# GpSimd issues the transfers of its own weights, and its second vector's product has a tile apart from the staging tile

## The chip, the core and the metric

The kernel is one program on one core of a Trainium2 chip. The core has five engines with an instruction queue each: TensorE (PE in the profile; PEld are its weight loads), VectorE (DVE), ScalarE (ACT), GpSimd (POOL) and SyncE (SP). Transfers between the chip's memory (HBM) and the on-chip memory (SBUF) run on 16 DMA engines, and an instruction in the queue of one of the engines starts each of them. The metric is device time in microseconds for one execution, smaller is better. For the kernel before, three runs gave 1352.70, 1353.47 and 1354.14 us, with a median of 1353.47 us.

## The reference

Two blocks of two layers each run one after the other on 256 tokens of width 1024, all in fp32. In both blocks a conditioning vector makes a shift, a scale and a gate for the channels; this is the *modulation*, and it is the part of the computation that the change touches.

```python
def hybrid_layer(x, c_silu, ...):                  # block 1, two layers
    mod = c_silu @ w_ada + b_ada                   # one vector x [1024, 3072]
    shift, scale, gate = jnp.split(mod, 3, axis=-1)
    u = rms_norm(x, norm_g) * (1 + scale[:, None]) + shift[:, None]
    z = u @ w_in                                   # then three attentions with their gates
    ...
    return x + gate[:, None] * (merged @ w_out)

def mixer_layer(x, cx, c, c_ctx, ...):             # block 2, two layers
    shift, scale, gate = jnp.split(jax.nn.silu(c) @ w_ada + b_ada, 3, axis=-1)
    shift_c, scale_c, gate_c = jnp.split(jax.nn.silu(c_ctx) @ w_ada + b_ada, 3, axis=-1)
    h = x * (1.0 + scale[:, None]) + shift[:, None]
    hc = cx * (1.0 + scale_c) + shift_c
    ...                                            # h @ w_in, hc @ w_in, then four mixers A, B, C, D
    x_new = layer_norm(alpha * x + gate[:, None] * (y @ w_out), ln_g, ln_b)
```

In block 1 one vector goes through `w_ada`, in block 2 two of them do (that of the tokens and that of the context).

## The kernel before, in words

Activations lie in SBUF with channels on the 128 partitions. The large products are fp32-exact by splitting: `raw` (L215 to L224) brings half a weight tile, [128, 4, 256] or 512 KB, into one of three buffers `wr` by a DMA on SP's queue (L222); `wtile` (L226) splits it into a rounded half `wh` (ACT, L114) and a remainder `wl` (DVE, L115); and TensorE makes three products per slice (L107) into PSUM. A load may be issued when a `wr` buffer is free, which is when the `wl` of the tile three loads earlier is done. All loads stand in the one queue of SP and are issued in its order.

The modulation products are background work. `ada` (L289) makes two sorts of it: `job` (TensorE multiplies the weights by the vector) and `wide` (L317), which leaves the multiplication to GpSimd. A `wide` fetches four chunks of 512 KB into `wsp` tiles (L324), and per chunk and 128-row slice GpSimd scales the slice by one entry of the vector (L330 the first, L333 the others) and adds it to the accumulator `acc` (L334). With two vectors (block 2) the first vector's product needs a tile of its own, `wc`, while the second's overwrites the weights. The `wsp` tiles take turns in a list of tags, `N.spare`: two buffers, `t3a` and `t3b` (L1373), which the jobs at the very start have used before, and eight where layer 2 of block 1 begins (`fill`, L256 and L539). `wc` lies in the tag `stg`, which has one buffer and is also the staging tile of `queries` and `quads` (L450, L461); these fill it on ACT and DVE and send it on by DMA.

When the accumulator is full, `end` (L336) lets TensorE sum over the partitions (`acc` against `ones`) and DVE write the result to `mod` (L342). `run_later` (L245) puts that 6 or 10 weight tiles after the wide. There are ten wides, six with one vector and four with two, so L324 stands for 40 transfers.

Two other things stand in GpSimd's queue: the `pow` operations of the norms, among them that of `rstd_row` (L379). At the start of a layer of block 1, DVE writes `rc` (L378), GpSimd raises it (L379), DVE makes the diagonal `dg` from it (L382), TensorE spreads it (L107), DVE copies it to `rstd` (L385) and scales the activations (L524), ACT writes `uh` (L525), and with that the layer's first projection can begin.

The order in each engine's queue is not the order of the Python code alone: the program is built with a scheduler that simulates engines and queues while it places instructions (`schedule_with_timeline_sim=True`, L1487), so an edit in one place can move instructions in another. The last part of the program that the prediction speaks of is mixer C of block 2 (`diff`, L1000), whose softmax per head alternates between TensorE, DVE (L482, L1019 to L1021) and ACT (L487, L497).

Of the kernel before, what the change touches and what calls it, by code (L numbers as in the profile page):

```python
# [58 lines left out]
class Net:  # L59
# [229 lines left out]
    def ada(self, l, blk):  # L289

        nc = self.nc
        nv = 1 if blk == 1 else 2
        wa = self.I["w_ada" if blk == 1 else "w_ada_2"][l]
        v0 = blk - 1
        mod = self.const.tile([128, 24, nv], F32, name=f"mod{blk}{l}")

        def load(n):
            return [self.raw(wa, k, n * 256, 256, True) for k in (0, 4)]

        def job(n, ws=None):  # L300
            ws = ws or load(n)
            bias = self.colB[:, 48 * (blk - 1) + 24 * l:48 * (blk - 1) + 24 * l + 24]
            p = self.P(self.pj, [128, 512])
            for k in range(8):
                g = 32 * (k % 4)
                self.mm(p[g:g + 32, :256], self.cs[:, k, :], ws[k // 4][:, k % 4, :], start=k < 4, stop=k >= 4)
            sb = self.W("adas", [128, 256], tag="score")
            nc.scalar.activation(sb, p[:, :256], AF.Copy)
            pc = self.P(self.tr, [128, 2, 4, 32])
            for j in range(2):  # L310
                self.T(pc[:, j].rearrange("p g v -> p (g v)"), sb[:, 128 * j:128 * j + 128])
            r = self.W("adar", [128, 2, nv])
            nc.vector.tensor_reduce(r, pc[:, :, :, v0:v0 + nv].rearrange("p j g v -> p j v g"), axis=AX.X, op=OP.add)
            nc.vector.scalar_tensor_tensor(mod[:, 2 * n:2 * n + 2, :], r, 0.5,
                                           bias[:, 2 * n:2 * n + 2][:, :, None].to_broadcast([128, 2, nv]),
                                           op0=OP.mult, op1=OP.add)
        def wide(n, tag):  # L317

            P = nc.gpsimd
            acc = self.K("acc", [128, 2, 512], tag=tag)  # L320
            for c in range(4):
                w = self.K("wsp", [128, 2, 512], tag=self.spare[self.nspare % len(self.spare)])
                self.nspare += 1
                nc.sync.dma_start(out=w, in_=wa[256 * c:256 * c + 256, 512 * n:512 * n + 512].rearrange(  # L324
                    "(k p) n -> p k n", p=128))
                for k in range(2):
                    for v in range(nv):
                        m = self.cs[:, 2 * c + k, v0 + v:v0 + v + 1]
                        if c == k == 0:
                            P.tensor_scalar(acc[:, v], w[:, k], m, None, op0=OP.mult)  # L330
                        else:
                            t = self.W("wc", [128, 512], tag="stg") if v + 1 < nv else w[:, k]
                            P.tensor_scalar(t, w[:, k], m, None, op0=OP.mult)  # L333
                            P.tensor_tensor(acc[:, v], acc[:, v], t, op=OP.add)  # L334

            def end():  # L336
                p = self.P(self.tr, [128, 4, 32])
                for j in range(4):
                    for v in range(nv):
                        self.mm(p[:, j, v:v + 1], acc[:, v, 128 * j:128 * j + 128], self.ones[:, 0:1])  # L340
                bias = self.colB[:, 48 * (blk - 1) + 24 * l:48 * (blk - 1) + 24 * l + 24]
                nc.vector.scalar_tensor_tensor(mod[:, 4 * n:4 * n + 4, :], p[:, :, :nv], 0.5,  # L342
                                               bias[:, 4 * n:4 * n + 4][:, :, None].to_broadcast([128, 4, nv]),
                                               op0=OP.mult, op1=OP.add)
            self.later.append((6 if nv == 1 else 10, end))

        return (mod, [lambda ws=None, n=n: job(n, ws) for n in range(12)], [lambda n=n: wide(n, ("s4", "w1")[n % 2]) for n in range(6)],
                load)

# [1142 lines left out]
```

## Time and profile before

| | |
|---|---|
| median of three runs | 1353.47 us (1352.70 to 1354.14) |
| the profiled execution | 1352.58 us, of which its span is 1350.8 us |
| TensorE busy | 1277.5 us, 95% of the span |
| VectorE busy | 908.9 us, 67% |
| ScalarE busy | 648.8 us, 48% |
| GpSimd busy | 393.9 us, 29%, nearly all of it before 660 us |
| mean granted TensorE clock | 0.972 of full speed |
| DMA | 217.65 MB in the span |

The trace is of one execution. Its span runs from the first instruction to the last, and 1.78 us of the execution lie around it. That execution was 0.89 us faster than the median. A sum made against the profiled execution therefore starts from 1352.6 us. Busy shares are averages over stages with different limits, so the rows below are read by stretches of the span.

### The profile page before, as it was taken

The page shows a single profiled execution, that of the slowest core. Times are in us where ns is not written, and L with a number is a line of the kernel's source. Part 1 is how long each engine was busy: PE and PEld are TensorE (multiplying, and loading weights), DVE is VectorE, ACT ScalarE, POOL GpSimd, SP SyncE. Part 2 cuts the span into 40 slices and gives each one's busy share as a digit, 9 for nine tenths or more (in the row PEclk, how much of TensorE's full clock was granted, in tenths as well). Part 3 has the DMA queues.
Part 4 walks back from the last instruction along what each step waited for, and adds up shares of the span by engine and source line. Part 5 has one row for each costly group of instructions (what it writes and reads, how often), then busy time and mean ns, then how long its engine had stood idle before and what let it go on. Part 6 is the DMA issues. An engine that isn't in the chain of part 4 may idle for free.

```text
span 1350.8 us, 27852 instructions
## 1 busy us (share of the span) xinstructions
PE 1277.5 (95%) x11386; PEld 1163.7 (86%) x11386; DVE 908.9 (67%) x1717; ACT 648.8 (48%) x1160; POOL 393.9 (29%) x233
## 2 busy tenths in 40 slices
PE   6999999999998999999998999999899999999986
PEld 2988988999898898899997988987789789999775
DVE  3897675665679855486675376754748768696873
ACT  3445456644444545764453233334736646434652
POOL 0484984150098921949500010000000000000000
PEclk8899999999989999999998999999899998999997
DMA  9764885476645575446664554326244255654220
GB/s 327 252 203 141 250 244 166 137 243 211 179 143 170 150 209 161 141 155 209 208 208 142 155 157 133 91 94 172 77 142 140 74 161 156 188 159 109 79 79 32
DMA packets 199599, 217.65 MB, mean 161 GB/s; under 512 B 10800, under 2 KB 183472, under 8 KB 198832
## 3 DMA queue, kind: packets, MB, share of 16 engines
q1 hardware_dynamic: 199472, 215.87, 53.2%
q8 instruction: 90, 1.47, 0.5%
q14 instruction: 37, 0.30, 0.1%
HBM read 199.06 MB, written 4.19 MB: 150 GB/s over the span
## 4 chain that ended last, share of the span: by engine, by line
PE 72%; DVE 12%; issue 6%; SPq 4%; DMA 3%; ACT 3%; POOL 0%; POOLq 0%; ACTq 0%; DVEq 0%
PE ps L107 68%; PE ps L111 4%; DVE wl L115 3%; SPq L466 2%; DMA wr<-w_in 2%; SPq L222 1%; DVE pe L703 1%; DVE nm L482 1%; DVE score L589 1%; ACT pe L487 1%; DMA wsp<-w_ada 1%; ACT wh L114 1%; DVE m L588 1%; DVE ro L428 1%; DVE score L584 0%
## 5 line engine op out<-in xcount | busy, mean ns | idle before, releaser
L115 DVE TENSOR_TENSOR wl<-wr,wh 128x1024 fp32r<-128x1024 f32 (+1 forms) x270 | 357.6, 1326 | 226.9 <-ACT wh L114 223.3
L114 ACT ACTIVATE wh<-wr 128x1024 fp32r<-128x1024 f32 (+1 forms) x270 | 284.9, 1056 | 349.3 <-PE ps L107 200.0
L107 PE MATMUL ps<-uh,wh 128*128 128x256 f32 x704 | 201.8, 287 | 3.4 <-ACT thm L659 3.4
L107 PE MATMUL ps<-ul,wh 128*128 128x256 f32 x704 | 201.2, 286 | 0.0
L107 PE MATMUL ps<-uh,wl 128*128 128x256 f32 x704 | 200.7, 285 | 0.0
L333 POOL TENSOR_SCALAR wsp<-wsp,cs 128x512 f32<-128x512 f32 x70 | 137.3, 1967 | 20.9 <-DMA wsp<-w_ada 20.9
L107 PEld LDWEIGHTS ps<-uh,wh 128*128 128x128 f32 x704 | 132.8, 189 | 5.8 <-ACT thm L659 4.4
L107 PEld LDWEIGHTS ps<-ul,wh 128*128 128x128 f32 x704 | 132.7, 188 | 3.1 <-issue 2.9
L107 PEld LDWEIGHTS ps<-uh,wl 128*128 128x128 f32 x704 | 132.8, 189 | 1.5 <-issue 1.1
L107 PE MATMUL ps<-wh,uh 128*128 128x256 f32 (+1 forms) x416 | 121.3, 293 | 1.8 <-ACT uh L525 1.4
L107 PE MATMUL ps<-wl,uh 128*128 128x256 f32 (+1 forms) x416 | 121.0, 292 | 1.5 <-DVE wl L115 1.5
L107 PE MATMUL ps<-wh,ul 128*128 128x256 f32 (+1 forms) x416 | 120.4, 290 | 0.4 <-DVE ul L526 0.4
L334 POOL TENSOR_TENSOR acc<-acc,wsp 128x512 f32<-128x512 f32 x70 | 107.8, 1540 | 2.5
L487 ACT ACTIVATE pe<-ps,nm 128x512 f32<-128x512 f32 (+2 forms) x160 | 85.0, 542 | 42.3 <-DVE nm L482 29.3
L397 POOL TENSOR_TENSOR rec<-rec,mhalf 128x8 f32<-128x8 f32 (+1 forms) x10 | 15.4, 1544 | 293.9 <-DVE rec L396 193.8
L482 DVE TENSOR_REDUCE nm<-ps 128x1 f32<-128x512 f32 (+2 forms) x104 | 70.8, 685 | 26.3 <-PE ps L107 24.7
L107 PEld LDWEIGHTS ps<-wh,uh 128*128 128x128 f32 x416 | 82.1, 198 | 3.7 <-ACT uh L525 1.6
L107 PEld LDWEIGHTS ps<-wl,uh 128*128 128x128 f32 x416 | 82.2, 198 | 2.8 <-DVE wl L115 1.8
L107 PEld LDWEIGHTS ps<-wh,ul 128*128 128x128 f32 x416 | 82.1, 198 | 0.8 <-DVE ul L526 0.7
L379 POOL TENSOR_TENSOR rc<-rc,mhalf 128x2 f32<-128x2 f32 x6 | 5.0, 833 | 255.4 <-DVE rc L378 255.4
L107 PE MATMUL ps<-wl,hxh 128*128 128x256 f32 x256 | 73.2, 286 | 0.5 <-DVE wl L115 0.5
L107 PE MATMUL ps<-wh,hxh 128*128 128x256 f32 x256 | 73.2, 286 | 0.1
(377 smaller groups left out, 3526.3 us busy)
## 6 DMA issues: line engine op xcount, KB each, us to landing
wr<-w_in SPq DMA_DIRECT2D x204, 512.0 KB, 4.1
wsp<-w_ada SPq DMA_DIRECT2D x68, 512.0 KB, 5.0
wr<-w_out SPq DMA_DIRECT2D x40, 512.0 KB, 3.5
wr<-w_ada SPq DMA_DIRECT2D x28, 512.0 KB, 4.5
wr<-w_br_a SPq DMA_DIRECT2D x8, 512.0 KB, 3.6
wr<-w_br_c SPq DMA_DIRECT2D x8, 512.0 KB, 4.0
wr<-w_br_b SPq DMA_DIRECT2D x8, 512.0 KB, 4.3
kC<-stg SPq DMA_DIRECT2D x64, 64.0 KB, 2.1
```

What stands on the lines that cost most here:

```text
L107: self.last_mm = self.nc.tensor.matmul(o, l, r, start=start, stop=stop, skip_group_check=True).ins
L111: self.nc.tensor.transpose(o, i, self.ident[:n, :n])
L114: self.nc.scalar.activation(h, x, AF.Copy)
L115: self.nc.vector.tensor_tensor(l, x, h, op=OP.subtract)
L222: self.nc.sync.dma_start(out=w[:, :, :n], in_=ap[k0 * 128:k0 * 128 + 512, c0:c0 + n].rearrange("(k p) n -> p k n", p=128))
L333: P.tensor_scalar(t, w[:, k], m, None, op0=OP.mult)
L334: P.tensor_tensor(acc[:, v], acc[:, v], t, op=OP.add)
L397: self.nc.gpsimd.tensor_tensor(r, r, self.mhalf[:, :r.shape[1]], op=OP.pow)
L428: V.tensor_tensor(dst, t1, b, op=OP.add)
L466: self.nc.sync.dma_start(out=d[32 * i:32 * i + 32].bitcast(F32), in_=g[32 * j:32 * j + 32, part].bitcast(F32))
L482: nc.vector.tensor_reduce(nmx, p, axis=AX.X, op=OP.max, negate=True)
L487: nc.scalar.activation(e[:, j, :], p[:, j, :], AF.Exp, bias=nm[:, h:h + 1], accum_out=ss[:, h:h + 1])
```

## The change

The transfers of `wide` are issued from GpSimd's queue instead of SP's, and `wc` gets the tag `w2` in the pool of long-lived tiles. That tag is otherwise used once, by a tile of the second layer of block 2.

```diff
             for c in range(4):
                 w = self.K("wsp", [128, 2, 512], tag=self.spare[self.nspare % len(self.spare)])
                 self.nspare += 1
-                nc.sync.dma_start(out=w, in_=wa[256 * c:256 * c + 256, 512 * n:512 * n + 512].rearrange(
+                P.dma_start(out=w, in_=wa[256 * c:256 * c + 256, 512 * n:512 * n + 512].rearrange(
                     "(k p) n -> p k n", p=128))
...
-                            t = self.W("wc", [128, 512], tag="stg") if v + 1 < nv else w[:, k]
+                            t = self.K("wc", [128, 512], tag="w2") if v + 1 < nv else w[:, k]
                             P.tensor_scalar(t, w[:, k], m, None, op0=OP.mult)
                             P.tensor_tensor(acc[:, v], acc[:, v], t, op=OP.add)
```

The three places in the order of the instructions on which the prediction rests follow. A row has the number on its engine, the line, the operation, the tiles it writes and reads, and in the first two pieces the semaphores that it waits for (DMAHW a transfer issued by SP, DMASW one issued by GpSimd, the others engines).

GpSimd's queue at the start of the program, before the change (`rc` is the norm's small tile, `wsp` a weight chunk, `acc` the accumulator):

```order
7 L379 TENSOR_TENSOR rc<-rc,mhalf 128x2 [waits DVE_49]
8 L330 TENSOR_SCALAR acc<-wsp,cs 128x512 [waits DMAHW6_49]
9 L333 TENSOR_SCALAR wsp<-wsp,cs 128x512 [waits DMAHW1_49,DMAHW0_49,PE_49]
10 L333 TENSOR_SCALAR wsp<-wsp,cs 128x512 [waits DMAHW2_49,DMAHW7_49,DMAHW1_49,PE_49]
11 L333 TENSOR_SCALAR wsp<-wsp,cs 128x512
12 L334 TENSOR_TENSOR acc<-acc,wsp 128x512 [waits Pool_49] x3
```

And after it:

```order
7 L379 TENSOR_TENSOR rc<-rc,mhalf 128x2 [waits DVE_49]
8 L324 DMA wsp<-w_ada 128x2x512 [waits DMAHW1_49,DMAHW0_49,PE_49]
9 L324 DMA wsp<-w_ada 128x2x512 [waits DMAHW2_49,DMAHW1_49,PE_49]
10 L330 TENSOR_SCALAR acc<-wsp,cs 128x512 [waits DMASW0_49]
11 L333 TENSOR_SCALAR wsp<-wsp,cs 128x512
12 L333 TENSOR_SCALAR wsp<-wsp,cs 128x512 [waits DMASW1_49]
13 L333 TENSOR_SCALAR wsp<-wsp,cs 128x512
14 L334 TENSOR_TENSOR acc<-acc,wsp 128x512 [waits Pool_49] x2
15 L324 DMA wsp<-w_ada 128x2x512
```

The first two transfers now stand right behind the first `pow` and wait only for the jobs that used `t3a` and `t3b`, no longer for the loads that stood ahead of them in SP's queue; later transfers stand between GpSimd's own operations.

GpSimd's queue where block 1's second layer begins, before the change:

```order
72 L334 TENSOR_TENSOR acc<-acc,wsp 128x512 [waits Pool_49] x3
73 L379 TENSOR_TENSOR rc<-rc,mhalf 128x2 [waits DVE_49]
74 L330 TENSOR_SCALAR acc<-wsp,cs 128x512 [waits DMAHW0_49,PE_49]
75 L330 TENSOR_SCALAR acc<-wsp,cs 128x512
76 L333 TENSOR_SCALAR wc<-wsp,cs 128x512 [waits DMAHW6_49,DMAHW7_49,DMAHW5_49,Activation_49]
```

And after it:

```order
108 L334 TENSOR_TENSOR acc<-acc,wsp 128x512 [waits Pool_49] x3
109 L324 DMA wsp<-w_ada 128x2x512 [waits DMAHW0_49,PE_49]
110 L324 DMA wsp<-w_ada 128x2x512 [waits DMAHW2_49,PE_49,Pool_49]
111 L379 TENSOR_TENSOR rc<-rc,mhalf 128x2 [waits DVE_49]
112 L330 TENSOR_SCALAR acc<-wsp,cs 128x512 [waits DMASW0_49]
113 L330 TENSOR_SCALAR acc<-wsp,cs 128x512
114 L333 TENSOR_SCALAR wc<-wsp,cs 128x512
```

Two transfers now stand ahead of the norm's `pow` in GpSimd's queue, and they wait for TensorE; and the first `wc` no longer waits for the three transfers out of the staging tile.

VectorE's queue in mixer C of the last layer, before the change (L482, L1019, L1020 and L1021 are the softmax of a head, L115 is the `wl` of a weight tile):

```order
1302 L1020 SCALAR_TENSOR_TENSOR dc<-ss,nlam,dc 128x1
1303 L482 TENSOR_REDUCE nm<-ps 128x1
1304 L1021 SCALAR_TENSOR_TENSOR pe<-pe,dc 128x512
1305 L482 TENSOR_REDUCE nm<-ps 128x1
1306 L1019 RECIPROCAL dc<-ss 128x1
1307 L1020 SCALAR_TENSOR_TENSOR dc<-ss,nlam,dc 128x1
1308 L482 TENSOR_REDUCE nm<-ps 128x1
1309 L1021 SCALAR_TENSOR_TENSOR pe<-pe,dc 128x512
```

And after it:

```order
1304 L1021 SCALAR_TENSOR_TENSOR pe<-pe,dc 128x512
1305 L482 TENSOR_REDUCE nm<-ps 128x1
1306 L115 TENSOR_TENSOR wl<-wr,wh 128x1024
1307 L1019 RECIPROCAL dc<-ss 128x1
1308 L1020 SCALAR_TENSOR_TENSOR dc<-ss,nlam,dc 128x1
1309 L482 TENSOR_REDUCE nm<-ps 128x1
1310 L1021 SCALAR_TENSOR_TENSOR pe<-pe,dc 128x512
1311 L482 TENSOR_REDUCE nm<-ps 128x1
1312 L115 TENSOR_TENSOR wl<-wr,wh 128x1024
```

Weight tiles are now split between the heads. TensorE's queue has the counterpart: before, the last eight of the fourteen gaps between the heads' score products hold no projection product; now six of these eight hold 3 to 14 each, 66 in all, which stood further ahead.

## Rows read from the trace of the kernel before

**Rows 1.** Busy time of an engine, its share of the span and its instructions.

```profile
PE 1277.5 (95%) x11386; PEld 1163.7 (86%) x11386; DVE 908.9 (67%) x1717; ACT 648.8 (48%) x1160; POOL 393.9 (29%) x233
```

**Rows 2.** Busy time by stretch: us, each engine (instructions), granted clock, DMA share, GB/s.

```profile
45.00:120.00 75.00, 72.04 (x567) 66.99 (x566) 69.13 (x127) 34.48 (x67) 55.53 (x33) 0.98 0.64 191
120.00:290.00 170.00, 167.98 (x1347) 156.27 (x1348) 105.85 (x148) 93.14 (x155) 101.59 (x57) 1.00 0.66 200
...
400.00:470.00 70.00, 65.86 (x515) 59.02 (x514) 66.48 (x119) 33.52 (x68) 65.38 (x38) 1.00 0.51 151
470.00:660.00 190.00, 187.06 (x1518) 176.61 (x1517) 113.84 (x150) 102.10 (x157) 116.81 (x66) 1.00 0.60 178
```

**Rows 3.** SP queue's waits: line, waited for, us in total, times, longest.

```profile
SPq L324 <- POOL acc L334: 57.7, 23, 6.8
```

**Rows 4.** Waits of all engines: the one of GpSimd for the staging tile.

```profile
POOL wc L333 <- DMA bq<-stg: 47.6, 1, 47.6
```

**Rows 5.** Costliest groups, GpSimd's two: count, busy, mean ns, idle before.

```profile
L333 POOL TENSOR_SCALAR wsp<-wsp,cs 128x512 f32<-128x512 f32 x70 | 137.3, 1967 | 20.9 <-DMA wsp<-w_ada 20.9
...
L334 POOL TENSOR_TENSOR acc<-acc,wsp 128x512 f32<-128x512 f32 x70 | 107.8, 1540 | 2.5
```

**Rows 6.** Timeline of GpSimd, end of the last accumulation: start us, us.

```profile
657.60 1.30 POOL L334 TENSOR_TENSOR acc<-acc,wsp 128x512 f32<-128x512 f32 x1
```

**Rows 7.** Timeline of TensorE, that accumulator's sum over the partitions.

```profile
678.69 1.84 PE L107 MATMUL ps<-ones,acc 128*128 128x1 f32 x16
```

**Rows 8.** Timeline of SP's queue at the start.

```profile
37.58 1.51 SPq L324 DMA_DIRECT2D wsp<-w_ada  x2
39.18 18.23 SPq L222 DMA_DIRECT2D wr<-w_in  x5
...
59.27 0.37 SPq L222 DMA_DIRECT2D wr<-w_in  x1
```

**Rows 9.** Timeline of TensorE at the start.

```profile
28.21 1.08 PE L107 MATMUL ps<-wsp,cs 128*32 128x256 f32 x8
...
30.48 1.94 PE L107 MATMUL ps<-wsp,cs 128*32 128x256 f32 x16
...
36.36 0.58 PE L107 MATMUL ps<-wl,uh 128*128 128x256 f32 x1 [1.48 <-DVE wl L115]
```

**Rows 10.** Busy time by stretch at the start.

```profile
30.00:35.00 5.00, 3.90 (x22) 1.49 (x22) 2.22 (x9) 2.22 (x5) 0.00 (x0) 0.50 1.09 349
```

**Rows 11.** Timeline of GpSimd at the start.

```profile
45.99 1.84 POOL L330 TENSOR_SCALAR acc<-wsp,cs 128x512 f32<-128x512 f32 x1 [26.50 <-DMA wsp<-w_ada]
```

**Rows 12.** Timeline of VectorE, two splits without and with GpSimd at work.

```profile
38.15 2.35 DVE L115 TENSOR_TENSOR wl<-pre,wh 128x1024 fp32r<-128x1024 f32 x2
...
54.73 4.51 DVE L115 TENSOR_TENSOR wl<-wr,wh 128x1024 fp32r<-128x1024 f32 x2
```

**Rows 13.** Timeline of all engines where block 1's second layer begins.

```profile
366.93 0.88 SPq L324 DMA_DIRECT2D wsp<-w_ada  x2
...
367.88 0.16 DVE L378 TENSOR_SCALAR rc<-ps 128x2 f32<-128x2 f32 x1 [1.18 <-PE ps L107]
368.12 0.73 POOL L379 TENSOR_TENSOR rc<-rc,mhalf 128x2 f32<-128x2 f32 x1 [78.45 <-DVE rc L378]
...
371.70 0.51 PE L107 MATMUL ps<-wh,uh 128*128 128x256 f32 x2 [1.36 <-ACT uh L525]
```

**Rows 14.** Busy time by stretch in the last layer's mixers.

```profile
1265.00:1280.00 15.00, 12.90 (x81) 9.60 (x81) 12.64 (x27) 11.37 (x27) 0.00 (x0) 1.00 0.22 70
```

**Rows 15.** Timeline of TensorE in mixer C of the last layer.

```profile
1273.24 1.10 PE L107 MATMUL ps<-vC,pt 128*128 128x64 f32 x8
1274.16 0.47 PE L107 MATMUL ps<-kC,qCx 128*128 128x512 f32 x1
...
1275.53 0.50 PE L107 MATMUL ps<-kC,qCx 128*128 128x512 f32 x1 [0.15 <-ACT pe L487]
1276.06 1.10 PE L107 MATMUL ps<-vC,pt 128*128 128x64 f32 x8
```

## The prediction

> **What bounds the kernel now.** I read the busy times first: TensorE works 1277.5 us, 95% of the span, and GpSimd 393.9, 29% [rows 1]. So an edit on GpSimd and SP can gain only where TensorE stands idle, and I looked at the stretches in which GpSimd accumulates [rows 2]. The reader is to see how little TensorE loses there: 2.96 us in 45 to 120, 2.02 in 120 to 290, 4.14 in 400 to 470 and 2.94 in 470 to 660, 12.1 us in all. That is the most that any relief of SP's queue could give, whatever else causes these losses. In 400 to 470 two other engines are full too, DVE with 66.48 and GpSimd with 65.38 of 70 us.
>
> Then the waits. SP's queue stands 57.7 us, in 23 waits, at L324, because a `wsp` buffer is still being multiplied [rows 3]; every `wr` load behind it is late by that much. It is the wait that the change takes away from SP. But the three `wr` buffers lie between, and in 120 to 290, where GpSimd accumulates for 101.59 us, TensorE is busy 167.98 of 170. GpSimd stands 47.6 us, once, for the staging tile [rows 4]. What waits for GpSimd there is only its own accumulator, and that is not in a hurry: the last one is complete at 658.9 us (657.60 + 1.30) [rows 6] and TensorE sums it at 678.69 [rows 7], 19.8 us later; it is the tightest of the ones I compared.
>
> **The price of an issue.** The trace holds no transfer issued by GpSimd. An issue on SP took 0.37 us [rows 8]; that is the lower end. GpSimd's smallest operation, on 128x2 elements, took 0.73 us [rows 13], so every instruction there carries a fixed part; 0.37 + 0.73 = 1.1 us is my value. A full GpSimd operation on 512 columns averages 1.97 us [rows 5], an upper end if writing an issue costs as much as computing. Further off lies the case that GpSimd stays with a transfer until it has landed: the pair issued at 37.58 let GpSimd start at 45.99 [rows 8, 11], 8.4 us for two, so 4.2 us each.
>
> **The change part by part**, against the profiled execution's 1352.6 us (its span of 1350.8 and 1.8 around it; 0.9 under the median).
>
> *SP's queue freed.* 40 issues leave SP: 40 x 0.37 = 15 us of its time, beside the 57.7 us of waits. Cover: the `wr` buffers, and SP would next wait for `wl` instead of for GpSimd. Value 0; the gain's end is the idle time above, worked out as a rival.
>
> *The tile `wc` off the staging tag.* 47.6 us of GpSimd wait go; they lie in the stretch before an accumulator that has tens of microseconds. Value 0.
>
> *Issues between GpSimd's own operations.* Four per wide, 4 x 1.1 = 4.4 us, against a slack of at least 19.8 us. Value 0. If an issue cost 4.2 us, four would take 16.8 us, which is still inside.
>
> *A, the start of the program: +1.5 us (0 to +5.2).* In SP's queue the first two transfers stood behind the first weights and the constants and went out at 37.58 [rows 8]. Now they need only the jobs that used the two buffers, which end at 29.3 and about 32 us (28.21 + 1.08; 30.48 + 1.94) [rows 9]. There the DMA engines are full, 349 GB/s [rows 10], with the loads that the first projections wait for. Two transfers of 0.524 MB are 1.05 MB / 349 GB/s = 3.0 us. If all of it came ahead of the first weights, the projections would begin 3.0 us later; with alternating packets half of that; 0 if the wait for DVE at 36.36 [rows 9] covers it. I take half. GpSimd's first products then come at about 36 to 38 instead of 45.99 [rows 11] and meet the first splits on DVE. Two splits took 2.35 us with GpSimd idle and 4.51 us with it at work [rows 12], 2.2 us more; that is added to the upper end alone, because the same meeting takes place later in the kernel before.
>
> *B, the layer boundary: +1.0 us (0 to +7.2).* SP issued the two transfers of the next wide at 366.93 (TensorE frees the buffer), and GpSimd was free for `rc` at 368.12, right behind DVE's write at 367.88 [rows 13]. Now both issues stand ahead of `rc`: 366.93 + 2 x 1.1 = 369.1, so `rc` begins 1.0 us later. Queued behind it are `dg`, the sum on TensorE, `rstd`, `uh` and the projection at 371.70, which had no other work to hide in. At 0.37 us an issue is over by 367.7 and costs nothing; at 1.97 it is 366.93 + 3.94 - 368.12 = +2.75; at 4.2, +7.2.
>
> *C, mixer C of the last layer: -2.1 us (-4 to +2).* From 1265 to 1280 TensorE is busy 12.90 of 15 us, DVE 12.64 [rows 14]. A head takes 2.82 us (1273.24 to 1276.06), and TensorE waits in it for ACT's exponentials [rows 15]. Now 66 projection products lie in these gaps. The idle 2.10 us are filled by work that stood in a stretch without idle time, so they come off the end. The busy figures of waiting products may hide as much again: -4. Against it: each head has a split of 1.2 us (half of the 2.35) more on DVE, 2.82 to 4.0 us per head; 28 products fill about that, but the last two heads are bare as before. If DVE sets the pace and the products don't cover it, two heads lose 1 us each: +2.
>
> *D, 400 to 470: -1.0 us (-3 to +1).* DVE has 95% there, slowed by GpSimd as in [rows 12]. Eight issues, 8.8 us, in which GpSimd writes no tile, spread its work thinner; part of the stretch's 4.14 idle TensorE us comes back. I take a quarter.
>
> Sum: 1.5 + 1.0 - 2.1 - 1.0 = -0.6, so 1352.0 by the profiled execution, 1352.9 by the median. I forecast 1352.4: no change that can be told.
>
> Two rules of the Trainium skill stand against or beside this. The rows show DVE and GpSimd slowing each other [rows 12]. The page "SBUF — State Buffer", section "SBUF: two separate sides", says more: a transfer issued from GpSimd has its descriptors written by GpSimd, and while DVE runs an operation that takes both port pairs these can't be written, so such loads belong in SP's or ACT's queue. No run so far shows it for an issue. At the boundary it would hold an issue up by a short operation of DVE, 0.48 us at the longest, for a sum of about -0.1 in place of -0.6; it gets no weight of its own. And "DMA: Bandwidth & Descriptors", section "Issuing engines are not separate DMA queues", says that another issuing engine saves only the time that the queue takes to issue. TensorE's 167.98 of 170 us with a blocked SP agree, and by it the freed queue is worth 0, as above.
>
> **The rivals.**
>
> 1. *GpSimd's issues hold up the norm (slower).* B with an issue near 4.2 us instead of 1.1. For it: GpSimd's waits behind two issues in one queue, and nothing else to do on TensorE. Against: SP's own 0.37. It decides from about 3.2 us an issue: 366.93 + 6.4 - 368.12 = +5.2, so 1352.0 + 4.2 = 1356.2. At 4.2 the time is 1352.0 - 1.0 + 7.2 = 1358.2; if the start goes the same way (A at +3), 1359.7. Chance 0.18.
> 2. *Thinner contention (faster).* The idle 4.14 us of 400 to 470 all come back: 1352.0 - 3.1 = 1348.9. For it: both engines full there; against: the work of GpSimd is the same, only later. Chance 0.13.
> 3. *SP was the limit after all (faster).* Half of the 7.9 us lost in the other three stretches comes back: 1352.0 - 4 = 1348.0. For it the 57.7 us; against it the full TensorE and the DMA share of 0.6. Chance 0.12.
> 4. *The heads don't gain.* DVE's splits cost what the filling gives, C at +2: 1352.0 + 4.1 = 1356.1. Chance 0.07.
>
> **How the numbers follow.** The forecast has 0.50, its own range 1349 to 1356. About 0.2%, 2.7 us, can be told from no change: faster is under 1350.8, slower over 1356.2. Of the forecast's 0.50, 0.38 is no change, 0.09 faster, 0.03 slower; rivals 2 and 3 are faster; rival 1 gives 0.15 slower and 0.03 no change, rival 4 gives 0.04 and 0.03. Faster 0.34, no change 0.44, slower 0.22. The range of 1346 to 1358.5 takes in both faster rivals and rival 1 up to its price of 4.2 us, and leaves some 0.08 below and 0.10 above.
>
> **What would show it.** The idle of TensorE in 120 to 290 and 470 to 660 should stay near 2 and 3 us with the wait of 57.7 us gone from SP's queue, and SP's waits for `wl` grow. At the start, GpSimd's first product should begin at 36 to 38 us, the first projection up to 3 us later. At the boundary the rows give the price directly: two issues, then `rc`; if `rc` begins within 0.3 us behind DVE's write, B is wrong, if 4 us behind it, rival 1 is right. In mixer C of the last layer TensorE should be full but for two heads. The wait for the staging tile should be gone without a trace on TensorE. The forecast is wrong if TensorE's sums over `acc` wait for GpSimd, or if DVE's splits grow beside GpSimd's issues.

## The result: slower by 1.0%

| | kernel before | changed kernel |
|---|---|---|
| median | 1354.14 us (5 runs, 1352.70 to 1355.08) | 1369.89 us (5 runs, 1361.28 to 1375.52) |
| ratio | | 1.010, 95% interval 1.0075 to 1.0124 |
| profiled execution, its span | 1352.58, 1350.8 us | 1361.28, 1359.1 us |
| mean granted TensorE clock | 0.972 | 0.970 there; 0.962 to 0.970 over the five |

I forecast 1352.4 us and a range up to 1358.5; that was wrong. The changed kernel is not only slower, it scatters: its five executions lie 14 us apart, those of the kernel before 2.4 us. The profiled one is the fastest of the five, so its trace shows only a part of the loss; the experiments show the rest. A ratio here and below is taken over the runs within 1.5% of their kernel's fastest, so it can differ from the quotient of the medians, which are of all runs; a trace of a run beyond that is not used.

The page of the changed kernel, its busy times, its new DMA queue and GpSimd's transfers (packets, MB and share; then count, KB, us from issue to landing):

```profile
PE 1280.4 (94%) x11386; PEld 1167.7 (86%) x11386; DVE 899.0 (66%) x1717; ACT 647.1 (48%) x1160; POOL 424.3 (31%) x273
...
q0 software_dynamic: 5760, 20.97, 5.1%
...
wsp<-w_ada POOLq DMA_DIRECT2D x40, 512.0 KB, 5.1
```

Busy time by stretch, to compare with [rows 2], and the largest wait of SP's queue:

```profile
120.00:290.00 170.00, 168.19 (x1328) 154.72 (x1327) 98.90 (x151) 94.26 (x164) 90.46 (x63) 0.99 0.63 185
470.00:660.00 190.00, 187.03 (x1498) 175.10 (x1497) 118.55 (x160) 103.55 (x165) 132.12 (x82) 0.99 0.60 177
```

```profile
SPq L222 <- DVE wl L115: 533.5, 179, 16.7
```

The same wait in the kernel before:

```profile
SPq L222 <- DVE wl L115: 483.3, 180, 13.2
```

The change does what it says: 40 transfers left SP, and their wait of 57.7 us [rows 3] is gone. It was worth nothing in the two stretches where GpSimd accumulates and TensorE is the busiest: TensorE is busy 168.19 of 170 and 187.03 of 190 us, after 167.98 and 187.06. SP waits instead for `wl`, 533.5 us against 483.3 before. (The stretches are of equal time, not of equal work; the later ones begin some 10 us of work earlier than in [rows 2].)

**Where the time goes.** ACT writes a `wh` tile 274 times, and I set the beginnings of these splits in one trace beside those in the other. Up to the first (33 us) the traces agree within 0.2 us. Between the 1st and the 11th, 33 to 61 us in the kernel before, the changed kernel loses 8.9 us. To the 93rd (359 us) it loses 5.3 more, to the 126th (496 us, with the boundary and the rope of layer 2) it gains 2.8, and to the 271st (1311 us) it gains 2.3.

Most of the 5.3 us go at 110 to 120 us, where the granted clock is 0.50 for 10.2 us, behind a stop of TensorE of 2.17 us. In the kernel before TensorE stops at the same work for 1.57 us, and no such fall follows. This part comes and goes with the execution: three of the kernels below (issue only, late product, first four on SP) have the same 10.2 us and lose 3.8 to 5.0 us between these splits; a repeat of the changed kernel has none and loses nothing there; the kernel with the tile alone has 6.8 us of it and loses 1.1.

The start first. GpSimd and DVE, then TensorE, each from its timeline (start, duration, what is written and read, idle time before and what ended it):

```profile
29.97 0.91 POOL L324 DMA_DIRECT2D wsp<-w_ada  x1 [10.19 <-DMA wsp<-w_ada]
32.22 0.73 POOL L324 DMA_DIRECT2D wsp<-w_ada  x1 [1.34 <-PE ps L107]
36.88 3.03 POOL L330 TENSOR_SCALAR acc<-wsp,cs 128x512 f32<-128x512 f32 x1 [3.94 <-DMA wsp<-w_ada]
...
49.37 0.77 POOL L324 DMA_DIRECT2D wsp<-w_ada  x1
```

```profile
48.21 1.51 DVE L115 TENSOR_TENSOR wl<-pre,wh 128x272 fp32r<-128x272 f32 x1
49.65 1.88 DVE L191 TENSOR_TENSOR nlam<-lamsm 128x1 f32<-128x1 f32 x2
51.45 0.68 DVE L428 TENSOR_TENSOR ro<-ro,rt 128x512 f32<-128x512 f32 x1
```

The same three of DVE in the kernel before, and TensorE in the changed one:

```profile
45.96 0.43 DVE L115 TENSOR_TENSOR wl<-pre,wh 128x272 fp32r<-128x272 f32 x1
46.31 0.65 DVE L191 TENSOR_TENSOR nlam<-lamsm 128x1 f32<-128x1 f32 x2
46.88 0.68 DVE L428 TENSOR_TENSOR ro<-ro,rt 128x512 f32<-128x512 f32 x1
```

```profile
52.28 1.08 PE L111 MATMUL ps<-ident,ro 128*128 128x128 f32 x4 [2.31 <-DVE nlam L193]
```

An issue takes 0.91 or 0.73 us. The first two go out at 29.97 and 32.22, against 37.58 [rows 8], and GpSimd multiplies from 36.88 on, 9 us earlier than in [rows 11]. That is as forecast. DVE then is late in its chain of small operations: `ro` (L428) begins at 51.45, and TensorE stands 2.31 us for it (the row names `nlam`, a neighbour of `ro` on DVE; the products read `ro`). In the kernel before, the same `ro` began at 46.88 and TensorE didn't stand. The 4.6 us have two causes. The constants landed later, behind the two transfers (the last of them at 45.41 against 43.07). And DVE's operations ran beside GpSimd's: the small `wl` at 48.21 took 1.51 us, 0.43 before; the two `nlam` 1.88 us, 0.65 before. One of the `nlam`, at 49.65, began inside the issue of the third transfer (49.37) and was let in only behind the accumulation that followed it: 1.7 of the 4.6 us hang on an issue and the operation behind it, not on a product.

What I hadn't counted is what follows the stop. Busy time by stretch again, granted clock third from the right, and below it one row of the kernel before:

```profile
50.00:55.00 5.00, 2.72 (x14) 2.75 (x14) 4.35 (x8) 1.54 (x2) 3.48 (x4) 0.72 0.69 180
55.00:60.00 5.00, 5.00 (x25) 5.00 (x25) 2.55 (x4) 1.06 (x1) 5.00 (x4) 0.50 0.75 239
60.00:65.00 5.00, 5.00 (x25) 5.00 (x25) 1.16 (x1) 1.09 (x2) 4.92 (x4) 0.50 0.34 105
65.00:70.00 5.00, 5.00 (x28) 5.00 (x27) 2.71 (x5) 0.86 (x3) 3.10 (x4) 0.57 0.68 209
```

```profile
55.00:60.00 5.00, 5.00 (x32) 5.00 (x32) 4.97 (x6) 1.72 (x3) 3.08 (x2) 0.66 0.57 170
```

After the stop TensorE is busy without a gap, but the granted clock is 0.50 (1.2 GHz of 2.4) for 17.1 us, up to 69 us. In the kernel before, it was at that level for 3.4 us between 55 and 60. The 13.7 us more cost about half of that, 6.8 us; with the 2.3 us of the stop that is the loss of 9 us. The other traces agree: behind stops of 2.59 and 3.70 us at this place (issue only, the changed kernel again) the clock is low for 17.1 us too, and where TensorE doesn't stop there, for 3.4 to 6.8 us.

The layer boundary, timeline of all engines, to compare with [rows 13]:

```profile
381.18 1.49 POOL L324 DMA_DIRECT2D wsp<-w_ada  x2 [76.31 <-PE ps L107]
...
381.75 0.16 DVE L378 TENSOR_SCALAR rc<-ps 128x2 f32<-128x2 f32 x1 [1.18 <-PE ps L107]
...
382.69 0.75 POOL L379 TENSOR_TENSOR rc<-rc,mhalf 128x2 f32<-128x2 f32 x1
...
386.28 0.50 PE L107 MATMUL ps<-wh,uh 128*128 128x256 f32 x2 [1.58 <-ACT uh L525]
```

Two issues, 1.49 us, then `rc`, as the order said; GpSimd's `rc` begins 0.94 us behind DVE's, 0.24 before. From the first issue to the layer's first projection it is 5.10 us, 4.77 before: +0.3, where I had +1.0.

### The profile page after: what moved, and what is told of

It reads as the page before. It is cut to its first block, busy times and chain, and to the rows that moved or that the text cites. A ratio compares the mean times of both kernels' runs of the same rounds, so it can differ in the third digit from the quotient of the medians.

```text
span 1359.1 us, 27836 instructions
## 1 busy us (share of the span) xinstructions
PE 1280.4 (94%) x11386; PEld 1167.7 (86%) x11386; DVE 899.0 (66%) x1717; ACT 647.1 (48%) x1160; POOL 424.3 (31%) x273
## 4 chain that ended last, share of the span: by engine, by line
PE 70%; DVE 11%; DMA 6%; issue 5%; SPq 4%; ACT 3%; POOL 0%; POOLq 0%; ACTq 0%; DVEq 0%
PE ps L107 65%; DMA wr<-w_in 5%; PE ps L111 4%; DVE wl L115 4%; SPq L466 1%; SPq L222 1%; ACT wh L114 1%; DVE nm L482 1%; ACT pe L487 1%; DMA wsp<-w_ada 1%; DVE score L589 1%; DMA cb<-cb 0%; DVE ro L428 0%; DVE m L588 0%; DVE pe L703 0%
## 5 line engine op out<-in xcount | busy, mean ns | idle before, releaser
L115 DVE TENSOR_TENSOR wl<-wr,wh 128x1024 fp32r<-128x1024 f32 (+1 forms) x270 | 351.1, 1301 | 233.7 <-ACT wh L114 231.8
L333 POOL TENSOR_SCALAR wsp<-wsp,cs 128x512 f32<-128x512 f32 x70 | 142.2, 2037 | 16.5 <-DMA wsp<-w_ada 16.3
L482 DVE TENSOR_REDUCE nm<-ps 128x1 f32<-128x512 f32 (+2 forms) x104 | 70.9, 686 | 26.2 <-PE ps L107 25.3
L107 PE MATMUL ps<-wh,hxl 128*128 128x256 f32 x256 | 72.5, 283 | 0.0
```

Of the source, the lines that this page charges most:

```text
L107: self.last_mm = self.nc.tensor.matmul(o, l, r, start=start, stop=stop, skip_group_check=True).ins
L115: self.nc.vector.tensor_tensor(l, x, h, op=OP.subtract)
L482: nc.vector.tensor_reduce(nmx, p, axis=AX.X, op=OP.max, negate=True)
```

## The experiments

All ran in rounds with the kernel before on the same chip; a ratio is to that, with its 95% interval. The twelve kernels ran in three groups; the kernel before had medians of 1351.12, 1350.66 and 1349.62 us beside them.

Theory 1: the early first transfers cost the time (the start, as above). Theory 2: a transfer issued by GpSimd costs wherever it stands. Theory 3: the instruction order that the scheduler made of the change costs. A fourth cause, the new tile of `wc`, was tried first.

**First group: which half of the change, and how much of it is the start.** The two halves alone:

```diff
 # issue only (against the changed kernel)
-                            t = self.K("wc", [128, 512], tag="w2") if v + 1 < nv else w[:, k]
+                            t = self.W("wc", [128, 512], tag="stg") if v + 1 < nv else w[:, k]
 # tile only (against the kernel before)
-                            t = self.W("wc", [128, 512], tag="stg") if v + 1 < nv else w[:, k]
+                            t = self.K("wc", [128, 512], tag="w2") if v + 1 < nv else w[:, k]
```

> GpSimd issues the transfers, wc stays in the staging tag; the order on TensorE, DVE, ACT and SP is that of the changed kernel. Theory 1 (at the start GpSimd's early transfers and early products make DVE 4.6 us late, TensorE stops for 2.3 us at 50 us and then runs 17 us at half clock): the stop is there again, 1360 to 1375. Theory 2 (a transfer from GpSimd costs more wherever it stands) and theory 3 (the moved order of the instructions costs it): also 1360 to 1375. Only if the new tile of wc were the cause would it come back to 1352 to 1356.

Measured: 1362.46 us, ratio 1.0082 (1.0049 to 1.0116).

> wc in the tag w2, the transfers stay on SP. All three theories: no change against the kernel before, 1352 to 1356, with GpSimd's wait of 47.6 us for the staging tile gone. If the tile were the cause: 1360 or more.

Measured: 1351.31 us, ratio 0.9997 (0.9980 to 1.0015). The loss is the issuing's alone; the 47.6 us of [rows 4] were worth nothing.

The start was tried in two ways, by giving the first wide's four transfers back to SP, and by holding back its products:

```diff
 # first four on SP (against the changed kernel)
-                self.nspare += 1
-                P.dma_start(out=w, in_=wa[...
+                self.nspare += 1; self.nwide = getattr(self, "nwide", 0) + 1
+                (nc.sync if self.nwide <= 4 else P).dma_start(out=w, in_=wa[...
 # late product (against the changed kernel; late is written behind nlam, L193)
+        self.late = C.tile([128, 8], F32, name="late"); V.scalar_tensor_tensor(self.late, self.nlam[:, 1:2].to_broadcast([128, 8]), 0.0, self.cs[:, :, 0], op0=OP.mult, op1=OP.add)
-                        m = self.cs[:, 2 * c + k, v0 + v:v0 + v + 1]
+                        m = self.late[:, 2 * c + k:2 * c + k + 1] if n == 4 and blk == 1 and l == 0 else self.cs[:, 2 * c + k, v0 + v:v0 + v + 1]
```

> The changed kernel with the first wide's four transfers issued from SP again; 36 of 40 stay on GpSimd and the order on TensorE, DVE and ACT stays that of the changed kernel. Theory 1: GpSimd's first product starts near 46 us again, no stop of over 1 us on TensorE before 60 us, and the 9 us lost there come back: 1349 to 1357. Theory 2 (36/40 of the loss stays) and theory 3 (order unchanged): 1360 to 1375.

Measured: 1356.69 us, ratio 1.0067 (1.0038 to 1.0095), and between the 1st and the 11th split +1.3 us instead of +8.9.

> The changed kernel, all transfers from GpSimd at the same early place, but the first wide's products use a copy of the vector that DVE writes only after the constants' last operation, so GpSimd's products start near 49 us instead of 37. The late landing of the constants stays (DVE 2.3 us late), the meeting of GpSimd's products with DVE's operations before 50 us goes (the other 2.3 us). Theory 1 as the sum of both: the stop at 50 us shrinks to under 0.5 us, no 17 us at half clock, 1350 to 1358. Rival 1b (the late constants alone): the stop stays near 2 us and the time at 1360 to 1375. Theories 2 and 3: 1360 to 1375.

Measured: 1361.61 us, ratio 1.0061 (1.0030 to 1.0092), between those splits +1.1 us. DVE and the stretch of the stop:

```profile
47.81 0.43 DVE L115 TENSOR_TENSOR wl<-pre,wh 128x272 fp32r<-128x272 f32 x1
48.16 0.22 DVE L191 TENSOR_TENSOR nlam<-lamsm 128x1 f32<-128x1 f32 x2
48.30 0.68 DVE L428 TENSOR_TENSOR ro<-ro,rt 128x512 f32<-128x512 f32 x1
```

```profile
50.00:55.00 5.00, 5.00 (x48) 5.00 (x46) 4.42 (x6) 2.61 (x3) 5.00 (x3) 0.99 0.53 144
55.00:60.00 5.00, 5.00 (x24) 5.00 (x25) 3.02 (x6) 1.72 (x3) 4.92 (x4) 0.50 0.62 180
```

The small `wl` takes 0.43 us again and `nlam` 0.22, `ro` begins at 48.30, and TensorE is busy all of the time; the clock is at 0.50 in 55 to 60 us, as in the kernel before for part of it. `ro` is 1.4 us later than before: that is what the constants do alone; the other 3.2 us of its 4.6 are GpSimd's work. So the mechanism of the start is shown in part: the constants' lateness alone doesn't stop TensorE, and GpSimd's early work is needed for it. This run moves the products and the third issue alike and doesn't separate them. But theory 1 fails as the whole cause. The kernel with four transfers on SP ends just inside its expected time, but beside a kernel before of 1351.12 us; the one with the late product misses it; and both stay 0.6 to 0.7% slower with the start mended. In the trace of the kernel with four transfers on SP, 15.0 us are lost between the 93rd and the 126th split, 359 to 496 us in the kernel before.

**Second group: the order, or the issues.** A look at the orders had an unexpected answer. If only transfers 25 and 26, those ahead of `rc` at the layer boundary, are SP's, then TensorE, DVE and ACT have exactly the order of the kernel before, everywhere, the tail included. All the reordering hangs on these two. That lets order and issuer be separated, by one condition in the same line:

```diff
-                (nc.sync if self.nwide <= 4 else P).dma_start(out=w, in_=wa[...
+                (nc.sync if self.nwide in (25, 26) else P).dma_start(out=w, in_=wa[...              # boundary on SP
+                (nc.sync if self.nwide in (1,2,3,4,25, 26) else P).dma_start(out=w, in_=wa[...      # start and boundary on SP
+                (nc.sync if self.nwide not in (25, 26) else P).dma_start(out=w, in_=wa[...          # boundary only on GpSimd
```

> The changed kernel with two of the 40 transfers, those ahead of the norm's pow where block 1's second layer begins, on SP again. With that alone the order on TensorE, DVE and ACT is that of the kernel before, everywhere. Theory 3 (the order that these two give costs 0.6%, the place is the rope of layer 2 at 415 to 480 us, where TensorE stops 3 to 4 us) leaves only the loss of the start: ratio 1.001 to 1.005. Theory 2 (each transfer from GpSimd costs): 38/40 of the loss, 1.007 to 1.010.

Measured: 1373.96 us, ratio 1.0128 (1.0074 to 1.0181).

> As the one before, and the first wide's four transfers on SP too; 34 of 40 are issued by GpSimd. Theory 3 with theory 1: both causes gone, ratio 0.997 to 1.002, no stop over 2 us on TensorE before 60 us and in 400 to 480 us. Theory 2: 34/40 of the loss, 1.006 to 1.009. If the freed queue of SP gives anything it shows here, below 0.998.

Measured: 1363.87 us, ratio 1.0086 (1.0054 to 1.0118).

> Only the two transfers at the layer boundary on GpSimd, 38 on SP; the order on TensorE, DVE and ACT is that of the changed kernel. Theory 3: the loss of the order in full, ratio 1.004 to 1.009, with a stop of TensorE of 3 us or more in 400 to 480 us in executions that are slow. Theory 2: 2/40 of the loss, within 0.999 to 1.002.

Measured: 1354.27 us, ratio 1.0017 (0.9992 to 1.0042).

> The changed kernel once more, beside the three others on the same chip. All theories: ratio 1.007 to 1.011, with executions from 1355 to 1378.

Measured: 1369.07 us, ratio 1.0117 (1.0079 to 1.0155); TensorE's stop at the start is there again, 3.70 us long, and this execution also loses 10.4 us between the 93rd and the 126th split.

Theory 3 falls: the order of the kernel before with GpSimd's issues is slow, the changed order without them is not. The kernel with start and boundary on SP is the best one to look into, since its order is that of the kernel before and its 93rd split is 0.5 us behind it. To the 126th 12.9 us go. GpSimd, DVE and TensorE in the first half of that place, and behind them GpSimd and DVE of the kernel before at a split that meets two accumulations:

```profile
413.52 0.77 POOL L324 DMA_DIRECT2D wsp<-w_ada  x1
414.34 1.57 POOL L333 TENSOR_SCALAR wc<-wsp,cs 128x512 f32<-128x512 f32 x1
415.88 1.26 POOL L334 TENSOR_TENSOR acc<-acc,wsp 128x512 f32<-128x512 f32 x1
417.10 1.26 POOL L334 TENSOR_TENSOR acc<-acc,wc 128x512 f32<-128x512 f32 x1
418.35 3.04 POOL L333 TENSOR_SCALAR wsp<-wsp,cs 128x512 f32<-128x512 f32 x1
```

```profile
416.07 3.38 DVE L115 TENSOR_TENSOR wl<-wr,wh 128x1024 fp32r<-128x1024 f32 x1
419.37 0.68 DVE L428 TENSOR_TENSOR ro<-ro,rt 128x512 f32<-128x512 f32 x1
```

```profile
420.11 0.66 PE L111 MATMUL ps<-ident,ro 128*128 128x128 f32 x4 [4.54 <-DVE ro L428]
```

```profile
418.92 1.30 POOL L334 TENSOR_TENSOR acc<-acc,wsp 128x512 f32<-128x512 f32 x1
420.17 2.25 POOL L334 TENSOR_TENSOR acc<-acc,wc 128x512 f32<-128x512 f32 x1
```

```profile
419.08 2.22 DVE L115 TENSOR_TENSOR wl<-wr,wh 128x1024 fp32r<-128x1024 f32 x1
```

The split at 416.07 needs 1.22 us alone; here it took 3.38. GpSimd ran two accumulations back to back, 1.26 us each, as fast as without any neighbour, and DVE came in only behind them; it is GpSimd's third operation (3.04 us) that is stretched. In the kernel before the split was let in behind the first accumulation (2.22 us for it), and the second was stretched. `ro` waits behind the split, and TensorE 4.54 us for `ro`. Busy time by stretch around this and a second such place (a split of 4.64 us at 462.50):

```profile
410.00:420.00 10.00, 5.56 (x48) 5.36 (x46) 9.76 (x19) 4.45 (x6) 9.96 (x7) 1.00 0.37 107
420.00:430.00 10.00, 9.89 (x72) 9.90 (x73) 9.86 (x20) 3.69 (x5) 10.00 (x6) 0.83 0.55 158
...
460.00:470.00 10.00, 5.82 (x38) 4.47 (x36) 9.97 (x8) 2.91 (x8) 9.96 (x7) 0.93 0.17 40
470.00:480.00 10.00, 8.02 (x39) 7.22 (x39) 7.64 (x12) 3.85 (x9) 4.84 (x4) 0.56 0.51 171
```

TensorE is busy 5.56 and 5.82 of 10 us, and in the 10 us behind each the granted clock is 0.83 and 0.56.

That gave theory 5, and a number to count: the DVE operations that took over 1.15 us longer than the same operation usually takes at its shortest, up to 760 us.

| kernel | transfers issued by GpSimd | such operations | of these between the 93rd and the 126th split | loss there |
|---|---|---|---|---|
| before; tile only | 0 | 0; 0 | 0; 0 | 0; 0.0 us |
| boundary only | 2 | 1 | 0 | -0.2 us |
| the changed kernel, two traces | 40 | 6; 5 | 2; 4 | -2.8; +10.4 us |
| issue only | 40 | 7 | 4 | +10.4 us |
| late product | 40 | 5 | 1 | +2.0 us |
| first four on SP | 36 | 9 | 6 | +15.0 us |
| start and boundary on SP | 34 | 8 | 6 | +12.9 us |

In the kernel before, no DVE operation is held by more than 1.1 us, which is less than one GpSimd operation; with GpSimd issuing, up to 3.5 us, almost three of them. What a trace loses by it depends on where the held operations fall: with four of them in that place it is 10.4 us, with six 12.9 to 15.0. With one or two it is no more than the clock alone can do. Between these splits the granted clock is 0.50 for 10.2 us in the kernel before; in the first trace of the changed kernel for 3.4 us, and so it wins time in spite of two held operations; with the late product for 17.1 us.

**Third group: theory 5 against its rival.** The rival: GpSimd gets its chunks earlier and works without its pauses (one of 4.11 us, up to 438.53, in the kernel before). Two kernels split the issues by stretch, one leaves GpSimd the issue but not the weights, one has another issuer:

```diff
 # second stretch only / first stretch only
+                (nc.sync if self.nwide < 27 else P).dma_start(out=w, in_=wa[...
+                (nc.sync if self.nwide < 5 or self.nwide > 24 else P).dma_start(out=w, in_=wa[...
 # small issue: SP fetches 510 of 512 columns of transfers 27 to 40, GpSimd the other two
+                self.nspare += 1; self.nwide = getattr(self, "nwide", 0) + 1; e = 510 if self.nwide > 26 else 512
+                nc.sync.dma_start(out=w[:, :, :e], in_=src[:, :, :e]); (e < 512 and P.dma_start(out=w[:, :, e:], in_=src[:, :, e:]))
 # ACT's queue
+                nc.scalar.dma_start(out=w, in_=wa[...
```

> All weights from SP but for the last two of 512 columns of transfers 27 to 40 (two vectors, 370 to 490 us), which GpSimd fetches: 14 issues of GpSimd at the places of the changed kernel, with 1/256 of the bytes, and the order of the kernel before on TensorE, DVE and ACT. Theory 5 (GpSimd's own issue lets its next two or three operations run in a row without DVE getting between, so single DVE operations are held up to 3.4 us instead of at most 1.1 us; where DVE sets the pace TensorE stops 3 to 5 us and its clock falls): DVE operations held over 1.15 us in 400 to 490, ratio 1.003 to 1.009. Rival theory 6 (the chunks arrive earlier and GpSimd works without its pauses): SP still feeds it, so no such operation and 0.998 to 1.002.

Measured: 1359.32 us, ratio 1.0063 (1.0039 to 1.0087); 6 held operations, 4 of them and +7.8 us between the 93rd and the 126th split. Its software queue, GpSimd, and one of the held splits:

```profile
q0 software_dynamic: 448, 0.03, 0.1%
```

```profile
402.88 0.76 POOL L325 DMA_DIRECT2D wsp<-w_ada  x1
403.69 1.58 POOL L333 TENSOR_SCALAR wc<-wsp,cs 128x512 f32<-128x512 f32 x1
405.23 1.30 POOL L334 TENSOR_TENSOR acc<-acc,wsp 128x512 f32<-128x512 f32 x1
406.49 1.29 POOL L334 TENSOR_TENSOR acc<-acc,wc 128x512 f32<-128x512 f32 x1
407.75 3.06 POOL L333 TENSOR_SCALAR wsp<-wsp,cs 128x512 f32<-128x512 f32 x1
```

```profile
404.91 3.96 DVE L115 TENSOR_TENSOR wl<-wr,wh 128x1024 fp32r<-128x1024 f32 x1
```

With 0.03 MB from GpSimd instead of 21, and the weights from SP, the same picture: issue, product, then two accumulations back to back while a DVE split of 1.22 us takes 3.96. So the issue in GpSimd's queue is enough for it, without the bytes, an earlier chunk or a freed SP; and GpSimd isn't rid of its pauses (one is 11.36 us). The rival falls as the main cause. It isn't ruled out as a part: this kernel loses 0.63%, the next one, with the same fourteen issues for whole chunks, 1.03%, and their intervals hardly overlap.

> GpSimd issues only transfers 27 to 40, of the products with two vectors (370 to 490 us), the others are SP's; order of the kernel before on TensorE, DVE and ACT. Theory 5: most of the loss of e6, since this is the stretch in which DVE sets TensorE's pace: ratio 1.004 to 1.009. A loss in proportion to the number of issues would give 14/34 of 0.86%: 1.0035.

Measured: 1364.46 us, ratio 1.0103 (1.0081 to 1.0124); 7 held operations, 6 of them and +13.9 us between these splits. These 14 issues cost as much as all 40, and a little more than theory 5's 1.009 at most.

> The complement: GpSimd issues transfers 5 to 24, of the products with one vector after the first wide (60 to 290 us), the others are SP's; order of the kernel before. DVE operations held over 1.15 us may occur, but TensorE has projections to do there: theory 5 gives 0.999 to 1.003. In proportion to the number, 20/34 of 0.86%: 1.005.

Measured: 1348.99 us, ratio 0.9989 (0.9973 to 1.0006); 2 held operations, none of them between these splits, +0.2 us. Its stretch of 400 to 470, to compare with [rows 2]:

```profile
400.00:470.00 70.00, 65.77 (x512) 58.67 (x511) 67.53 (x120) 33.41 (x68) 65.02 (x39) 1.00 0.50 155
```

That is the stretch of the kernel before again, DVE at 67.53 of 70 us included. So theory 2 is right that GpSimd's issuing costs, and wrong that it does so wherever it stands: twenty issues in the first stretch cost nothing. Whether that is because TensorE has projections enough there, or because twenty issues held only two operations, no run separates. And an SP queue relieved of twenty transfers gains nothing that can be told.

> All 40 transfers issued from ACT's queue: SP is as free as in the changed kernel, GpSimd issues nothing; the order of instructions is another one again. Theory 5: no DVE operation held over 1.15 us, ratio 0.996 to 1.004. Theory 2 for any issuer but SP, or a freed SP queue that pulls weight loads into the transfers' way: 1.006 or more. If freeing SP's queue is worth something, below 0.998.

Measured: 1362.42 us, ratio 1.0100 (1.0074 to 1.0126). The time is a miss, but for another reason. No DVE operation is held, and from the 93rd to the 126th split 2.1 us are lost, with the clock low for 17.1 us as with the late product. GpSimd's own operations stand in another order than in the kernel before here, as they do in every kernel of this section, the one with the tile alone too; these two hold nothing, so a moved order on GpSimd is not enough for it. Most of what ACT's queue loses is at the start, where ACT's queue waits for the issue's turn (ACTq is its issuing):

```profile
37.91 0.44 ACTq L324 DMA_DIRECT2D wsp<-w_ada  x1
38.39 0.51 ACT L525 ACTIVATE uh<-af,mod 128x256 fp32r<-128x256 f32 x1 [7.61 <-DMA cf<-cf]
...
39.93 1.05 ACT L114 ACTIVATE wh<-wr 128x1024 fp32r<-128x1024 f32 x1
```

The first `wh` comes at 39.93 instead of 33 us, behind an issue that had to wait; the trace's whole loss at the last split is 12.0 us, 7 of them here. An issue holds up what stands behind it on its engine, and on ACT at the start that is the first weight split.

## Why the prediction was wrong, step by step

*SP's queue freed: value 0.* Right. Twenty transfers (0.9989), thirty-eight or forty off SP gave no gain that could be told, and TensorE's idle time in 120 to 290 and 470 to 660 us stayed at 2 and 3 us.

*`wc` off the staging tag: value 0.* Right, 0.9997.

*The price of an issue, 1.1 us.* Measured 0.72 to 0.91 us alone, 1.49 for two. The estimate served, though its fixed part was misread: four MEMSETs of GpSimd at the start of the kernel before took 0.10 us each, so not every operation there carries the 0.73 us of the `pow`.

*Issues between GpSimd's own operations: value 0.* **This step failed**, and with it *D*. I costed an issue as time on GpSimd against GpSimd's slack of 19.8 us, and that slack was real. But [rows 12] said that GpSimd's operations also take time from DVE, and I took that exchange as fixed. It isn't: with issues among its operations GpSimd holds DVE off for up to 3.5 us, almost three operations on end. In D I even gave the issues a gain, 1 us, for spreading GpSimd's work thinner. From the 93rd to the 126th split, six of eight traces with the fourteen issues lost 7.8 to 15.0 us; one lost 2.0, no more than ACT's kernel without any hold, and one, the profiled changed kernel, won 2.8. The fourteen issues alone cost 1.03% (1.0081 to 1.0124). The place was right, [rows 2] has DVE at 95% and TensorE idle there; the sign was wrong. The prediction had this among its signs of being wrong: DVE's splits grow beside GpSimd's issues, one from 1.22 to 4.64 us.

*A, the start: +1.5 us (to +5.2).* The mechanism was right, late constants and DVE beside GpSimd's earlier products (and one issue, which my sum had at nothing), and the stop of 2.3 us lies inside the range. What failed is the size: the term took a stop at its length. The granted clock of 0.50 behind it brought it to 8.9 us. The kernel before shows such a clock at its very start [rows 10], and I did not price it. Over whole runs the start is worth less sure a number: 1.0128 with the first four issues and 1.0086 without, with intervals that overlap.

*B, the boundary: +1.0 us.* +0.3 measured; rival 1 fell with an issue of 0.75 us.

*C, mixer C: -2.1 us.* The gaps were filled as the order said; busy time by stretch of the changed kernel, two stretches that cover most of the heads:

```profile
1260.00:1275.00 15.00, 15.00 (x126) 14.77 (x125) 11.70 (x22) 10.18 (x21) 0.00 (x0) 1.00 0.47 126
1275.00:1290.00 15.00, 13.87 (x94) 11.63 (x93) 11.51 (x24) 9.61 (x22) 0.00 (x0) 0.93 0.33 105
```

TensorE is full to 1275 and then idle 1.13 us, against 2.10 in [rows 14]. But the time isn't won: from the 241st to the 271st split the traces with the changed order run from 1.6 us won to 3.4 us lost (0.1 won in the one shown), and those with the order of the kernel before from 2.5 us won to 0.2 us lost. What this end gains or loses is not set by the filled gaps.

*Rival 1* had the right sign and the wrong place. *Rivals 2 and 3* fell. *Rival 4*, heads that gain nothing, came out in kind but not at its price: C is near 0 in place of -2.1, not at +2, and that isn't what made the kernel slower. The rule of the Trainium skill that I gave no weight ("SBUF — State Buffer", section "SBUF: two separate sides": loads issued from GpSimd meet DVE at the shared ports, issue them from SP or ACT) pointed the right way. Its mechanism, an issue held up by DVE, is not what the traces show: the issues keep to 0.7 to 0.9 us, and it is DVE that is held up. Nor did its way out help here: ACT's queue cost 1.0%, for the reason told above. Its other sentence, that the engine that starts first keeps the ports for the whole instruction, fits the 1.1 us of the kernel before; that an issue makes it two or three instructions, no run here explains.

## What to carry to other kernels

An issue put into the queue of a computing engine is not only its own 0.8 us: look at what that engine shares with the engine that sets the pace, and at what stands behind the issue. Where TensorE is fed by a chain without slack, price a stop by its length and by the clock behind it; here 2.3 us cost 9. And before crediting a freed queue, ask whether anything that was late in it ever stopped the bound engine.

## What the runs showed that I had not expected

- With transfer issues in GpSimd's queue a waiting DVE operation can be left out for two or three GpSimd operations: the longest hold of a trace is 1.8 to 3.5 us, against 1.1 to 1.2 us in the four kernels without such issues or with two. Of the 56 held operations 22 began during an issue or just behind it and were let in behind the next operation (1.3 to 1.8 us, the issue included), and 20 began within 3 us behind one (1.2 to 3.1 us). But 14 began later, 13 of them 5.8 to 13.3 us behind the last issue, the split at 462.50 among them. So it is not only the operations right behind an issue that run through. Why an issue has this effect stays open.
- The issuer of two transfers out of 40 decided the place of 1227 of the 11386 matmuls in TensorE's order, up to 1275 us. Taken alone that order was worth 0.17% with an interval across zero.
- The changed kernel scatters by 19.6 us in nine of eleven runs (1356.66 to 1376.25; the other two took 1381.24 and 1385.06), the kernel before beside it by 12.5 us in 22 runs: one profile of a kernel that scatters shows one draw.
